# Written order over attention, four high-part buffers, rotation in single slots, ScalarE copies of turned v

## The chip, the cores and the metric

One core of a Trainium2 chip runs the whole program. The metric is the device time of one execution in microseconds (us), as the median of repeated runs. A difference of about 0.2% (3.9 us here) is what a measurement of this kernel can tell from no change.

## What is computed

One layer of a streaming encoder, on T = 320 rows: 256 of a new prompt and 64 of a running sample. D = 2048, 32 query heads and 4 key/value heads of 64, feed-forward width 5632, all float32.

```python
xn = rmsnorm(x)
u, v, q, k, va = split(xn @ w_in)            # u, v through gelu
q, k = rope(q), rope(k)                       # the first 16 of 64 dimensions
a = u * (ws @ layernorm(v) + bs)              # per chunk of 128 rows
o = sink_softmax(q @ k.T / 8, sinks) @ va     # chunks of 64 rows, window of 3 chunks
x += (sigmoid(ga) * (a @ w_branch_a) + sigmoid(gb) * (o @ w_branch_b)) @ w_out
x += (silu(h @ w_ffn_gate) * (h @ w_ffn_up)) @ w_ffn_down     # h = rmsnorm(x)
y = rmsnorm(x)
```

`ga` and `gb` are `xn @ w_gate + b_gate`, halved. Outputs are y, the new rows of k and va, and the normalised v of the sample.

## The kernel before, in words

**Blocks.** Every float32 product is made of three products of rounded parts (high by high, high by low, low by high). The weights come in blocks of 256 rows by 512 columns (512 KB). For each block SP issues a transfer into a `raw` tile (`fetch`, L127), ScalarE (ACT) rounds it into `hi` (L135), VectorE (DVE) makes `lo = raw - hi` (L144), and TensorE (PE) does 24 matmuls with 320 columns (L168 to L170), one each 0.147 us where nothing holds it up: 3.52 us a block. `hi` and `lo` have three tiles each (`PARTS`), `raw` has four (`RAWS`). While block j is multiplied, the parts of block j + 2 are made, and `raw` of block j + 6 is fetched.

**Order of the products.** First k and va (`first_gemm`, blocks 0 to 7), then from block 8, eight blocks each: q0, q1, v0, q2, v1, q3, v2, v3, gate b (gb0 to gb3), then branch b, u, gate a, branch a, the output product and the feed-forward part. The list of rows below says mm_q, mm_v, mm_gb for these.

**Calendar.** `gemm` calls `pump()` after each half block, which runs what the calendar holds for that slot (1.76 us). `later(n, fn)` books n slots ahead. After each q product `q_done` copies it to `qr` (L641), swaps the rotated rows by four small transfers on ACT's queue (`rope_swap`, L367 and L368, `swp<-qr`), rotates (`rope_turn`, L375 to L377, three DVE operations on 128x640 each, with a temporary tile of tag "st"), and splits it into `qs` (ACT L508, DVE L512, two each).

**An attend.** For each of the four groups g and the five query chunks n there is one attend, named g_n, five slots after the one before. Its steps and slots are: scores (0: PE L524, L525 into two banks `s`), peak (1: DVE `mx` L533, `nm` L535), power (2: ACT, four exponentials L546), weigh (3, 4), pack (5: DVE transpose into `u`), spread (6: SP, four transfers `pd<-u`, L577), gather (8: SP, `pf<-pd`, L586), part (11: ACT `ph` L598 and `p2` L606; 12: DVE `pl` L601, `p2` L609), values (14: PE L616 into a bank `o`), lower (15: ACT `ol` L620) and total (16: DVE L628). `pf` and `ol` take turns in the two tiles of tag "st". The page prints `p2` as `p`.

**v.** After each v product `v_done` scales it (DVE L663), applies gelu (ACT L666), turns it on PE into a bank `vt` (L671) and copies the bank into `tok`: the 256 prompt columns on DVE (L676), the 64 sample rows on ACT (L677). Statistics follow on DVE.

**Banks.** All of these share eight PSUM banks under one tag: a product holds four, an attend's scores two, its values one, each turned v one. A new tile takes a bank that the program's order has released before, and PE waits there until the last reader of that bank is done.

**Who orders.** The start, up to the end of `first_gemm`, stands under `tc.manual_schedule()`: there each engine's queue has the order in which the code was written. After that the tile framework's scheduler orders each engine's instructions within the dependences. Each engine runs its queue in order, so whatever stands ahead of an instruction is done first.

Of the kernel before, what the change touches and what calls it, by code (L numbers as in the profile page):

```python
# [10 lines left out]
F32 = mybir.dt.float32  # L11
F32R = mybir.dt.float32r
AF = mybir.ActivationFunctionType
ALU = mybir.AluOpType
# [4 lines left out]
P = 128  # L19
D = 2048  # L20
DC = D // P
T = 320
# [3 lines left out]
W = 512  # L26
# [1 line left out]
NPOS = 128 + T  # L28
WARM = 9
FILL = (6, 4)  # L30
RAWS = 4
PARTS = 3
FPARTS = (16, 16, 12)
DOWN = [
    [(0, 4), (512, 4), (1024, 4), (1536, 4)],
# [35 lines left out]
def tile_hybrid_step(ctx: ExitStack, tc: tile.TileContext, a: dict, outs: list):  # L71
    nc = tc.nc
# [6 lines left out]
    wpool = ctx.enter_context(tc.tile_pool(name="wpool", bufs=1))  # L79
# [11 lines left out]
    def later(slots, fn):  # L91
        calendar.setdefault(now[0] + max(1, slots), []).append(fn)

    startup = tc.manual_schedule()
    startup.__enter__()

    def pump():
        now[0] += 1
# [3 lines left out]
    def flush():  # L102
        while calendar:
            pump()
# [15 lines left out]
    def fetch(j, pieces=1):  # L120
        if j < len(plan):
            w, c0, k, nt = plan[j]
            raws[j] = wpool.tile([P, 2, W], F32, tag="raw", name=f"raw_{j}", bufs=RAWS)
            src = w[k * P : (k + 2) * P, c0 : c0 + nt * P].rearrange("(c p) m -> p c m", p=P)
            n = 2 // pieces
            for c in range(0, 2, n):
                nc.sync.dma_start(raws[j][:, c : c + n, : nt * P], src[:, c : c + n, :])  # L127

    def high(j, eng=None):
        if j < len(plan):  # L130
            n = plan[j][3] * P
            hi = wpool.tile([P, 2, W], F32R, tag="hi", name=f"hi_{j}", bufs=PARTS)
            parts[j] = [hi]
            if eng is None:
                nc.scalar.activation(hi[:, :, :n], raws[j][:, :, :n], AF.Copy)  # L135
            else:
                eng.tensor_copy(hi[:, :, :n], raws[j][:, :, :n])

    def low(j):
        if j < len(plan):  # L140
            n = plan[j][3] * P
            lo = wpool.tile([P, 2, W], F32R, tag="lo", name=f"lo_{j}", bufs=PARTS)
            parts[j].append(lo)
            nc.vector.tensor_tensor(  # L144
                lo[:, :, :n], raws.pop(j)[:, :, :n], f32(parts[j][0][:, :, :n]), op=ALU.subtract
            )

    def prepare(j, eng=None):
        high(j, eng)
        low(j)  # L150

    def gemm(w, c0, xh, xl, name, k0=0, nk=DC, nt=4):
        ps = [bank(f"mm_{name}_{t}") for t in range(nt)]
        for kb in range(0, nk, 2):
            j = at_block[0]
            at_block[0] += 1
            assert plan[j][1:] == (c0, k0 + kb, nt)
            ahead = j + PARTS - 1
            todo = ahead not in parts
            if todo:  # L160
                high(ahead)
            hi, lo = parts.pop(j)
            for t in range(nt):
                cols = slice(t * P, (t + 1) * P)
                for c in range(2):
                    k = kb + c
                    o = ps[t][:, :T]
                    nc.tensor.matmul(o, hi[:, c, cols], xh[:, k, :], start=(k == 0), stop=False)  # L168
                    nc.tensor.matmul(o, hi[:, c, cols], xl[:, k, :], start=False, stop=False)  # L169
                    nc.tensor.matmul(o, lo[:, c, cols], xh[:, k, :], start=False, stop=(k == nk - 1))  # L170
                if t == 1:
                    if todo:
                        low(ahead)
                    fetch(ahead + RAWS)
                if t % 2 == 1:
                    pump()
        return [p[:, :T] for p in ps]
# [9 lines left out]
    tok = main.tile([P, 3, D], F32, name="tok")  # L187
# [108 lines left out]

    def first_block():

        hi = wpool.tile([P, 2, W], F32R, tag="hi", name="hi_0", bufs=PARTS)
        lo = wpool.tile([P, 2, W], F32R, tag="lo", name="lo_0", bufs=PARTS)  # L300
        raw = raws.pop(0)
        x_in(0)
        keep_warm(FILL[0])
        nc.vector.tensor_copy(hi[:, 0, :], raw[:, 0, :])
        nc.vector.tensor_tensor(lo[:, 0, :], raw[:, 0, :], f32(hi[:, 0, :]), op=ALU.subtract)
        x_in(1)
        keep_warm(FILL[1])
        nc.scalar.activation(hi[:, 1, :], raw[:, 1, :], AF.Copy)
        nc.vector.tensor_tensor(lo[:, 1, :], raw[:, 1, :], f32(hi[:, 1, :]), op=ALU.subtract)
        parts[0] = [hi, lo]  # L310
# [1 line left out]
    first_block()  # L312
    load_x(3, nc.sync)
    fetch(3)
    fetch(4)
    prepare(1)
    x_in(2)
    fetch(5)
    for k in range(DC):
        later(k + 1, lambda k=k: x_keep(k))  # L320
        if k + 3 < DC:
# [45 lines left out]
            nc.scalar.dma_start(swp[b : b + 8, 0:nt, :], qr[b + 8 : b + 16, 0:nt, :])  # L367
            nc.scalar.dma_start(swp[b + 8 : b + 16, 0:nt, :], qr[b : b + 8, 0:nt, :])  # L368

    def rope_turn(t0):  # L370
        t1 = tmp.tile([P, 2, T], F32, tag="st", name="rope_t1")
        cb = cos_t.unsqueeze(1).broadcast_to([P, 2, T])
        sb = sin_t.unsqueeze(1).broadcast_to([P, 2, T])
        q2 = qr[:, t0 : t0 + 2, :]
        nc.vector.tensor_tensor(q2, q2, cb, op=ALU.mult)  # L375
        nc.vector.tensor_tensor(t1, swp[:, t0 : t0 + 2, :], sb, op=ALU.mult)
        nc.vector.tensor_tensor(q2, q2, t1, op=ALU.add)  # L377

    ka = ap.tile([P, 4, NPOS], F32R, name="ka")
    kl = ap.tile([P, 4, NPOS], F32R, name="kl")  # L380
# [85 lines left out]
    def first_gemm():  # L466

        ps = [bank(f"mm_kv_{t}") for t in range(4)]
        for k in range(DC):
            j, c = k // 2, k % 2  # L470
            hi, lo = parts[j]
            for t in range(4):
                cols = slice(t * P, (t + 1) * P)
                o = ps[t][:, :T]
                nc.tensor.matmul(o, hi[:, c, cols], xh[:, k, :], start=(k == 0), stop=False)
                nc.tensor.matmul(o, hi[:, c, cols], xl[:, k, :], start=False, stop=False)
                nc.tensor.matmul(o, lo[:, c, cols], xh[:, k, :], start=False, stop=(k == DC - 1))
            pump()
            if c == 1:
                parts.pop(j)  # L480
                prepare(j + 2)
                fetch(j + 2 + RAWS)
        at_block[0] = DC // 2
        return [p[:, :T] for p in ps]

    ps = first_gemm()
    startup.__exit__(None, None, None)
    for t in range(4):
        nc.scalar.activation(qr[:, t, :], ps[t], AF.Copy)
    later(1, lambda: rope_swap(2))  # L490
# [1 line left out]
    for i, n in xs:  # L492
        later(7 + i, lambda i=i, n=n: new_v(i, i * P, n))
        later(9 + 2 * i, lambda i=i: v_blocks(i))
    later(8, lambda: rope_turn(0))
    later(11, k_out)
    later(11, rope_scale)
    for g in range(4):
# [17 lines left out]
    def attend(g, n, qs, st):  # L516
# [105 lines left out]
        def total():  # L622
# [10 lines left out]
        return (  # L633
            (0, scores), (1, peak), (2, power), (3, lambda: weigh((1, 3))), (4, lambda: weigh((0, 2))),
            (5, pack), (6, spread), (8, gather), (11, lambda: part(False)), (12, lambda: part(True)),
            (14, values), (15, lower), (16, total),
        )

    def q_done(g, ps):
        for t in range(4):  # L640
            nc.scalar.activation(qr[:, t, :], ps[t], AF.Copy)  # L641
        qs = ap.tile([P, 20, 2, 64], F32R, tag="qs", name=f"qs_{g}")
        hi, lo = q_parts(g, qs)
        later(1, lambda: rope_swap(4))
        later(5, lambda: rope_turn(0))
        later(7, lambda: rope_turn(2))
        at = QK0[g]
        later(at - 5, lambda: hi(0))
        later(at - 4, lambda: lo(0))
        later(at - 3, lambda: hi(1))  # L650
        later(at - 2, lambda: lo(1))
        for n in range(5):
            for dt, step in attend(g, n, qs, {}):
                later(at + 5 * n + dt, step)
# [4 lines left out]
    def v_done(g, ps):  # L659
        vst = {}  # L660
        for t in range(4):
            v = tmp.tile([P, T], F32, tag="e1", name=f"v_{g}_{t}", bufs=4)
            nc.vector.tensor_tensor(v, ps[t], rx, op=ALU.mult)  # L663

            def curve(v=v):
                nc.scalar.activation(v, v, AF.Gelu_apprx_tanh)  # L666

            def turn(t=t, v=v):
                pt = vst[t] = bank(f"vt_{g}_{t}")
                for i, n in xs:  # L670
                    nc.tensor.transpose(pt[:n, i * P : (i + 1) * P], v[:, i * P : i * P + n], ident)  # L671

            def put(t=t):
                pt = vst.pop(t)
                c = slice((4 * g + t) * P, (4 * g + t + 1) * P)
                nc.vector.tensor_copy(tok[:, 0:2, c], pt[:, 0:256].rearrange("p (i c) -> p i c", i=2))  # L676
                nc.scalar.activation(tok[0:64, 2, c], pt[0:64, 256:384], AF.Copy)  # L677

            later(1, curve)
            later(3 + t, turn)  # L680
            later(4 + t, put)

        def stats():
            for i, n in xs:
                nc.vector.bn_stats(bst[:n, i, g, :], tok[:n, i, g * W : (g + 1) * W])

        later(9, stats)
# [57 lines left out]
        if h == 1:  # L745
            nc.vector.memset(late["wst"][64:128, :, 0:64], 0.0)

    at = 19
    later(at - 2, open_late)
    for k in range(0, DC, 2):  # L750
        later(at - 2 + k // 2 + 1, lambda k=k: split_o(k))
# [24 lines left out]
    for g in range(1, 4):  # L776
        sigmoid(gate_b, gemm(w_gate, D + g * W, xh, xl, f"gb{g}"), 80, g)
    flush()
    yh, yl = late["yh"], late["yl"]
    for g in range(4):  # L780
        ps = gemm(w_bb, g * W, yh, yl, f"bb{g}")
# [234 lines left out]
```

## Time and profile before

| | |
|---|---|
| median of 3 runs | 1955.37 us (1954.38 to 1955.47) |
| the profiled execution | 1956.22 us |
| its span | 1954.0 us, granted clock 0.995 |
| PE busy | 1931.7 us, 99% |
| DVE, ACT busy | 1042.0 us (53%), 814.3 us (42%) |
| bytes moved | 307.41 MB, mean 157 GB/s |

The span is what the trace covers; 2.2 us of the profiled execution lie around it. PE's share says that nearly the whole time is matmul time, so a change to the other engines can only win what PE spends waiting or at a lower clock. Attention runs beside PE from about 50 to 330 us; there DVE and ACT have their fullest stretches (six to eight tenths of a slice, four or five later).

### The profile page before, as it was taken

What the parts mean: (1) busy time and instruction counts of PE and PEld (TensorE: products, weight loads), DVE (VectorE), ACT (ScalarE), POOL (GpSimd) and SP (SyncE); (2) the same over time, 40 slices, a digit from 0 to 9 for tenths busy, and PEclk for the clock granted to TensorE, in tenths of its full rate; (3) what the DMA queues carried; (4) which work ended last, traced back from release to release, by engine and by line L of the source; (5) the groups of instructions that cost most, each with busy time, mean ns of one, the idle gap of its engine ahead of it and who ended that gap; (6) DMA issues with size and microseconds to landing.
All of it is one profiled execution on the core that took longest, in us unless ns stands there. A gap on an engine that the chain in (4) does not pass through costs nothing.

```text
span 1954.0 us, 31842 instructions
## 1 busy us (share of the span) xinstructions
PE 1931.7 (99%) x13201; PEld 1925.1 (99%) x13201; DVE 1042.0 (53%) x1528; ACT 814.3 (42%) x1221; POOL 4.7 (0%) x12
## 2 busy tenths in 40 slices
PE   9999999999999999999999999999999999999997
PEld 9999999999999999999999999999999999999996
DVE  6878787944355544455554444443444444444454
ACT  6666776532333343334443333333333333333343
POOL 0000000000000000000000000000000000000000
PEclk9999999999999999999999999999999999999998
DMA  8566665644444454445455555445555444555433
GB/s 278 159 172 171 171 188 174 221 157 151 151 141 132 146 148 149 149 150 205 151 148 147 149 149 151 151 151 151 149 148 148 150 151 151 151 151 149 149 128 103
DMA packets 170881, 307.41 MB, mean 157 GB/s; under 512 B 11457, under 2 KB 31377, under 8 KB 170545
## 3 DMA queue, kind: packets, MB, share of 16 engines
q1 hardware_dynamic: 166064, 295.93, 49.6%
q10 hardware_dynamic: 4672, 9.46, 1.5%
q8 instruction: 103, 1.69, 0.3%
q14 instruction: 42, 0.34, 0.0%
HBM read 292.15 MB, written 12.45 MB: 156 GB/s over the span
## 4 chain that ended last, share of the span: by engine, by line
PE 83%; ACT 1%; DVE 1%; DMA 0%; issue 0%; DVEq 0%; SPq 0%; ACTq 0%
PE mm_fg L169 5%; PE mm_fd L169 5%; PE mm_fu L169 5%; PE mm_fd L168 5%; PE mm_fu L168 5%; PE mm_fg L168 5%; PE mm_fg L170 5%; PE mm_fu L170 5%; PE mm_fd L170 5%; PE mm_u L168 2%; PE mm_ba L170 2%; PE mm_bb L169 2%; PE mm_bb L168 2%; PE mm_wo L170 2%; PE mm_ga L170 2%; PE mm_ga L168 2%
## 5 line engine op out<-in xcount | busy, mean ns | idle before, releaser
L144 DVE TENSOR_TENSOR lo<-raw,hi 128x1024 fp32r<-128x1024 f32 (+1 forms) x533 | 645.1, 1211 | 659.8 <-ACT hi L135 658.3
L135 ACT ACTIVATE hi<-raw 128x1024 fp32r<-128x1024 f32 (+1 forms) x533 | 559.2, 1050 | 1013.8 <-PE mm_fu L169 188.9
L168 PE MATMUL mm_fd<-xh,hi 128*128 128x320 f32 x704 | 218.2, 310 | 0.0
L168 PE MATMUL mm_fg<-yh,hi 128*128 128x320 f32 x704 | 217.8, 309 | 0.0
L170 PE MATMUL mm_fg<-yh,lo 128*128 128x320 f32 x704 | 217.5, 309 | 0.0
L168 PE MATMUL mm_fu<-yh,hi 128*128 128x320 f32 x704 | 217.5, 309 | 0.0
L169 PE MATMUL mm_fu<-yl,hi 128*128 128x320 f32 x704 | 217.5, 309 | 0.0
L170 PE MATMUL mm_fu<-yh,lo 128*128 128x320 f32 x704 | 217.5, 309 | 0.0
L169 PE MATMUL mm_fg<-yl,hi 128*128 128x320 f32 x704 | 217.5, 309 | 0.0
L170 PE MATMUL mm_fd<-xh,lo 128*128 128x320 f32 x704 | 217.1, 308 | 0.0
L169 PE MATMUL mm_fd<-xl,hi 128*128 128x320 f32 x704 | 217.1, 308 | 0.0
L168 PEld LDWEIGHTS mm_fg<-yh,hi 128*128 128x128 f32 x704 | 132.1, 188 | 0.1
L169 PEld LDWEIGHTS mm_fg<-yl,hi 128*128 128x128 f32 x704 | 132.1, 188 | 0.1
L170 PEld LDWEIGHTS mm_fg<-yh,lo 128*128 128x128 f32 x704 | 132.1, 188 | 0.0
L168 PEld LDWEIGHTS mm_fu<-yh,hi 128*128 128x128 f32 x704 | 132.1, 188 | 0.0
L169 PEld LDWEIGHTS mm_fu<-yl,hi 128*128 128x128 f32 x704 | 132.1, 188 | 0.0
L170 PEld LDWEIGHTS mm_fu<-yh,lo 128*128 128x128 f32 x704 | 132.1, 188 | 0.0
L169 PEld LDWEIGHTS mm_fd<-xl,hi 128*128 128x128 f32 x704 | 132.1, 188 | 0.0
L168 PEld LDWEIGHTS mm_fd<-xh,hi 128*128 128x128 f32 x704 | 132.1, 188 | 0.0
L170 PEld LDWEIGHTS mm_fd<-xh,lo 128*128 128x128 f32 x704 | 132.1, 188 | 0.0
L168 PE MATMUL mm_q<-xh,hi 128*128 128x320 f32 x256 | 81.6, 319 | 0.0
L168 PE MATMUL mm_u<-xh,hi 128*128 128x320 f32 x256 | 80.3, 314 | 0.0
(262 smaller groups left out, 3935.8 us busy)
## 6 DMA issues: line engine op xcount, KB each, us to landing
raw<-in_w_in_dram SPq DMA_DIRECT2D x103, 512.0 KB
raw<-in_w_ffn_gate_dram SPq DMA_DIRECT2D x88, 512.0 KB
raw<-in_w_ffn_up_dram SPq DMA_DIRECT2D x88, 512.0 KB
raw<-in_w_ffn_down_dram SPq DMA_DIRECT2D x82, 512.0 KB
raw<-in_w_gate_dram SPq DMA_DIRECT2D x64, 512.0 KB
raw<-in_w_branch_b_dram SPq DMA_DIRECT2D x32, 512.0 KB
raw<-in_w_branch_a_dram SPq DMA_DIRECT2D x32, 512.0 KB
raw<-in_w_out_dram SPq DMA_DIRECT2D x32, 512.0 KB
```

The lines of the kernel that those rows point to most:

```text
L135: nc.scalar.activation(hi[:, :, :n], raws[j][:, :, :n], AF.Copy)
L144: nc.vector.tensor_tensor(lo[:, :, :n], raws.pop(j)[:, :, :n], f32(parts[j][0][:, :, :n]), op=ALU.subtract)
L168: nc.tensor.matmul(o, hi[:, c, cols], xh[:, k, :], start=(k == 0), stop=False)
L169: nc.tensor.matmul(o, hi[:, c, cols], xl[:, k, :], start=False, stop=False)
L170: nc.tensor.matmul(o, lo[:, c, cols], xh[:, k, :], start=False, stop=(k == nk - 1))
```

## The change

The order as written now lasts until the gate b products end (block 104): the `manual_schedule` is left there, not after `first_gemm`. In the code that it covers the following differs.

- `hi` has four tiles, `lo` three, `raw` three. Parts are still made two blocks ahead (`AHEAD`), and a block's transfer is issued one block later than before (j + 5 instead of j + 6); the start issues one block less.
- Rotation is done in place in `swp`, and its three operations stand in slots of their own: 8, 9, 10 for k (all at 8 before) and 3, 4, 5, 5, 6, 6 after a q product (before: all three of the first half at 5, of the second at 7).
- The copy of the turned prompt columns goes from DVE to ACT.
- `total` comes two slots later (18), and the late work after v (pools, normalisation) two slots later.

Line numbers of the changed kernel are 2 or 3 higher.

```diff
-RAWS = 4
-PARTS = 3
+RAWS = 3
+HIGHS = 4
+LOWS = 3
+AHEAD = 2
...
-            hi = wpool.tile([P, 2, W], F32R, tag="hi", name=f"hi_{j}", bufs=PARTS)
+            hi = wpool.tile([P, 2, W], F32R, tag="hi", name=f"hi_{j}", bufs=HIGHS)
...
-            lo = wpool.tile([P, 2, W], F32R, tag="lo", name=f"lo_{j}", bufs=PARTS)
+            lo = wpool.tile([P, 2, W], F32R, tag="lo", name=f"lo_{j}", bufs=LOWS)
...
-            ahead = j + PARTS - 1
+            ahead = j + AHEAD
...
     fetch(3)
-    fetch(4)
     prepare(1)
     x_in(2)
-    fetch(5)
+    fetch(4)
...
-    def rope_turn(t0):
-        t1 = tmp.tile([P, 2, T], F32, tag="st", name="rope_t1")
+    def rope_ops(t0):
...
-        q2 = qr[:, t0 : t0 + 2, :]
-        nc.vector.tensor_tensor(q2, q2, cb, op=ALU.mult)
-        nc.vector.tensor_tensor(t1, swp[:, t0 : t0 + 2, :], sb, op=ALU.mult)
-        nc.vector.tensor_tensor(q2, q2, t1, op=ALU.add)
+        q2, s2 = qr[:, t0 : t0 + 2, :], swp[:, t0 : t0 + 2, :]
+        return (
+            lambda: nc.vector.tensor_tensor(q2, q2, cb, op=ALU.mult),
+            lambda: nc.vector.tensor_tensor(s2, s2, sb, op=ALU.mult),
+            lambda: nc.vector.tensor_tensor(q2, q2, s2, op=ALU.add),
+        )
...
     ps = first_gemm()
-    startup.__exit__(None, None, None)
...
-    later(8, lambda: rope_turn(0))
+    for i, op in enumerate(rope_ops(0)):
+        later(8 + i, op)
...
-            (14, values), (15, lower), (16, total),
+            (14, values), (15, lower), (18, total),
...
-        later(5, lambda: rope_turn(0))
-        later(7, lambda: rope_turn(2))
+        a, b = rope_ops(0), rope_ops(2)
+        for dt, op in ((3, a[0]), (4, b[0]), (5, a[1]), (5, b[1]), (6, a[2]), (6, b[2])):
+            later(dt, op)
...
-                nc.vector.tensor_copy(tok[:, 0:2, c], pt[:, 0:256].rearrange("p (i c) -> p i c", i=2))
+                nc.scalar.activation(tok[:, 0:2, c], pt[:, 0:256].rearrange("p (i c) -> p i c", i=2), AF.Copy)
...
-    at = 19
+    at = 21
...
     flush()
+    ordered.__exit__(None, None, None)
     yh, yl = late["yh"], late["yl"]
```

**ACT's queue around the exponentials of attend 0_4** (block 33, the first v product; `qs_1` belongs to the next group's queries, `v_0_*` to the v product). Before:

```order
L620 ACTIVATE ol_0_1_1696<-o_0_1_1675 64x512
L598 ACTIVATE ph_0_2_1731<-pf_0_2_1638 128x512
L135 ACTIVATE hi_35_1711<-raw_35_1515 128x1024
L606 ACTIVATE p2_0_2_1733<-pf_0_2_1638 64x512
L508 ACTIVATE qs_1_1253<-qr_178 64x20x64 x2
L546 ACT_TABLE_LOAD
L546 ACTIVATE pr_0_4_1766,den_0_4_1767<-s_0_4_0_1701,nm_0_4_1742 128x192 x2
```

Now:

```order
L622 ACTIVATE ol_0_1_1688<-o_0_1_1667 64x512
L137 ACTIVATE hi_35_1703<-raw_35_1547 128x1024
L600 ACTIVATE ph_0_2_1721<-pf_0_2_1630 128x512
L608 ACTIVATE p2_0_2_1723<-pf_0_2_1630 64x512
L510 ACTIVATE qs_1_1247<-qr_176 64x20x64
L548 ACT_TABLE_LOAD
L548 ACTIVATE pr_0_4_1756,den_0_4_1757<-s_0_4_0_1693,nm_0_4_1732 128x192 x2
```

One of the two `qs` copies has moved behind the exponentials; everything else that stood ahead of them still does.

**DVE's queue ahead of `lo_49`** (block 47; attend 1_4 has its peak here, and `qs_2` is the next group's). Before:

```order
L609 TENSOR_TENSOR p2_1_2_2438<-pf_1_2_2359,p2_1_2_2438 64x512
L535 SCALAR_TENSOR_TENSOR nm_1_4_2447<-mx_1_4_2444,nsink_175 128x4
L512 TENSOR_TENSOR qs_2_2103<-qr_178,qs_2_2103 64x20x64
L537 TENSOR_TENSOR es_1_4_2449<-sink_174,nm_1_4_2447 128x4
L512 TENSOR_TENSOR qs_2_2103<-qr_178,qs_2_2103 64x20x64
L555 TENSOR_TENSOR den_1_4_2468<-den_1_4_2468,es_1_4_2449 128x4
L663 TENSOR_TENSOR v_1_0_2520<-mm_v1_0_2104,rx_118 128x320
L556 RECIPROCAL den_1_4_2468<-den_1_4_2468 128x4
L144 TENSOR_TENSOR lo_49_2489<-raw_49_2272,hi_49_2475 128x1024
```

Now:

```order
L537 SCALAR_TENSOR_TENSOR nm_1_4_2435<-mx_1_4_2432,nsink_173 128x4
L539 TENSOR_TENSOR es_1_4_2437<-sink_172,nm_1_4_2435 128x4
L603 TENSOR_TENSOR pl_1_2_2452<-pf_1_2_2349,ph_1_2_2424 128x512
L611 TENSOR_TENSOR p2_1_2_2426<-pf_1_2_2349,p2_1_2_2426 64x512
L514 TENSOR_TENSOR qs_2_2095<-qr_176,qs_2_2095 64x20x64
L146 TENSOR_TENSOR lo_49_2477<-raw_49_2324,hi_49_2463 128x1024
```

Only one `qs` low part is left ahead of `lo_49`, and the first scaling of v (L663, now L666) comes behind it.

**DVE's queue around the peak of attend 2_0** (blocks 49 and 50; `mx_2_0` reads its scores, `nm_2_0` goes to its exponentials). Before:

```order
L601 TENSOR_TENSOR pl_1_3_2609<-pf_1_3_2493,ph_1_3_2573 128x512
L533 TENSOR_REDUCE mx_2_0_2612<-s_2_0_0_2581 128x2
L144 TENSOR_TENSOR lo_51_2605<-raw_51_2382,hi_51_2591 128x1024
L609 TENSOR_TENSOR p2_1_3_2575<-pf_1_3_2493,p2_1_3_2575 64x512
L533 TENSOR_REDUCE mx_2_0_2612<-s_2_0_1_2582 128x2
L535 SCALAR_TENSOR_TENSOR nm_2_0_2615<-mx_2_0_2612,nsink_175 128x4
```

Now:

```order
L146 TENSOR_TENSOR lo_51_2593<-raw_51_2422,hi_51_2579 128x1024
L603 TENSOR_TENSOR pl_1_3_2597<-pf_1_3_2483,ph_1_3_2561 128x512
L611 TENSOR_TENSOR p2_1_3_2563<-pf_1_3_2483,p2_1_3_2563 64x512
L535 TENSOR_REDUCE mx_2_0_2600<-s_2_0_0_2569 128x2
L535 TENSOR_REDUCE mx_2_0_2600<-s_2_0_1_2570 128x2
L537 SCALAR_TENSOR_TENSOR nm_2_0_2603<-mx_2_0_2600,nsink_173 128x4
```

`lo_51` has moved to the front, so `pl` waits behind it; the same five instructions stand ahead of `nm_2_0` as before. On ACT `hi_51`, for which `lo_51` waits, still stands behind `ph_1_3`, and now behind `p2_1_3` too; ahead of `ph_1_3` stand now the table load for gelu and the four gelus of v1, in one run. On SP the gather `pf_1_3` follows `raw_52` now; before, it followed `raw_53`. With three `raw` tiles `raw_52` takes the tile that `lo_49` frees, as `raw_53` did with four.

## Rows read from the trace of the kernel before

**Rows 1.** The page: busy time of each engine; the chain that ended last, by engine.

```profile
PE 1931.7 (99%) x13201; PEld 1925.1 (99%) x13201; DVE 1042.0 (53%) x1528; ACT 814.3 (42%) x1221; POOL 4.7 (0%) x12
...
PE 83%; ACT 1%; DVE 1%; DMA 0%; issue 0%; DVEq 0%; SPq 0%; ACTq 0%
```

**Rows 2.** PE's waits: waiting line, releaser: us in total, times, longest us.

```profile
PE vt L671 <- ACT pr L546: 3.5, 3, 2.5
PE o L616 <- ACT pr L546: 2.0, 1, 2.0
...
PE s L524 <- DVE qs L512: 0.5, 1, 0.5
PE o L616 <- DVE p L609: 0.2, 1, 0.2
```

**Rows 3.** PE's timeline at 144 us: start, duration, operation [idle before <-releaser].

```profile
147.01 0.90 PE L671 MATMUL vt<-ident,v 128*128 128x128 f32 x3 [2.55 <-ACT pr L546]
```

**Rows 4.** PE's timeline at 215 us.

```profile
217.03 0.50 PE L616 MATMUL o<-ph,vv 128*128 128x512 f32 x1 [2.02 <-ACT pr L546]
```

**Rows 5.** Windows: length, busy us of each engine (instructions), granted clock, DMA share, GB/s.

```profile
147.01:150.08 3.07, 3.07 (x13) 3.03 (x13) 2.97 (x8) 3.02 (x11) 0.00 (x0) 0.51 0.43 128
160.00:163.07 3.07, 3.07 (x21) 2.94 (x20) 2.30 (x7) 2.56 (x9) 0.00 (x0) 1.00 0.81 261
217.03:221.30 4.27, 4.26 (x19) 4.04 (x20) 3.22 (x9) 3.82 (x14) 0.00 (x0) 0.65 0.28 73
20.00:30.00 10.00, 9.80 (x70) 9.54 (x69) 6.52 (x12) 6.48 (x13) 0.00 (x0) 1.00 0.98 324
```

**Rows 6.** ACT's timeline at 130 to 147 us (attend 0_4's exponentials at its end).

```profile
130.07 0.63 ACT L598 ACTIVATE ph<-pf 128x512 fp32r<-128x512 f32 x1 [2.28 <-DMA pf<-pd]
132.21 0.42 ACT L546 ACTIVATE pr<-s,nm 128x192 f32<-128x192 f32 x1 [1.51 <-DVE nm L535]
...
141.99 2.55 ACT L508 ACTIVATE qs<-qr 64x1280 fp32r<-64x1280 f32 x2
144.75 1.28 ACT L546 ACT_TABLE_LOAD   x1 [0.21 <-DVE nm L535]
146.05 0.42 ACT L546 ACTIVATE pr<-s,nm 128x192 f32<-128x192 f32 x1
```

**Rows 7.** DVE's timeline at 200 to 215 us (attends 1_3, 1_4, 2_0).

```profile
200.74 1.49 DVE L512 TENSOR_TENSOR qs<-qr,qs 64x1280 fp32r<-64x1280 f32 x1
...
202.45 1.49 DVE L512 TENSOR_TENSOR qs<-qr,qs 64x1280 fp32r<-64x1280 f32 x1
...
204.53 1.19 DVE L144 TENSOR_TENSOR lo<-raw,hi 128x1024 fp32r<-128x1024 f32 x1
...
214.72 0.16 DVE L535 SCALAR_TENSOR_TENSOR nm<-mx,nsink 128x4 f32<-128x4 f32 x1
```

**Rows 8.** SP's queue at 206 us.

```profile
205.76 0.39 SPq L127 DMA_DIRECT2D raw<-in_w_in_dram  x1
206.33 0.85 SPq L586 DMA_DIRECT2D pf<-pd  x2
```

**Rows 9.** ACT's timeline at 204 to 216 us.

```profile
202.89 1.06 ACT L135 ACTIVATE hi<-raw 128x1024 fp32r<-128x1024 f32 x1
203.97 1.28 ACT L666 ACT_TABLE_LOAD   x1
...
210.81 0.63 ACT L598 ACTIVATE ph<-pf 128x512 fp32r<-128x512 f32 x1 [1.73 <-DMA pf<-pd]
...
216.28 0.31 ACT L546 ACTIVATE pr<-s,nm 128x64 f32<-128x64 f32 x1
```

**Rows 10.** Groups by line, 8 to 560 us: count | busy us, mean ns | idle before, releaser.

```profile
L375 DVE TENSOR_TENSOR qr<-qr,cos_t 128x640 f32<-128x640 f32 x9 | 7.3, 813 | 1.2 <-DMA swp<-qr 1.2
...
L676 DVE COPY tok<-vt 128x256 f32<-128x256 f32 x16 | 6.6, 416 | 0.1
...
L428 ACT ACTIVATE kout<-pk 128x256 f32<-128x256 f32 x1 | 0.4, 359 | 0.0
```

More of the change, by code (lines that the diff above doesn't have):

```diff
@@ L92, in later @@
         calendar.setdefault(now[0] + max(1, slots), []).append(fn)
-    startup = tc.manual_schedule()
-    startup.__enter__()
+    ordered = tc.manual_schedule()
+    ordered.__enter__()
     def pump():
@@ L297, in first_block @@
     def first_block():
-        hi = wpool.tile([P, 2, W], F32R, tag="hi", name="hi_0", bufs=PARTS)
-        lo = wpool.tile([P, 2, W], F32R, tag="lo", name="lo_0", bufs=PARTS)
+        hi = wpool.tile([P, 2, W], F32R, tag="hi", name="hi_0", bufs=HIGHS)
+        lo = wpool.tile([P, 2, W], F32R, tag="lo", name="lo_0", bufs=LOWS)
         raw = raws.pop(0)
@@ L480, in first_gemm @@
                 parts.pop(j)
-                prepare(j + 2)
-                fetch(j + 2 + RAWS)
+                prepare(j + AHEAD)
+                fetch(j + AHEAD + RAWS)
         at_block[0] = DC // 2
```

## The prediction

> **What bounds the kernel now.** I read the page's busy times and chain first: PE is busy 99% of the span and is 83% of the chain that ended last, the other engines about 1% each [rows 1]. So the time is the matmuls, and a change to the order can only win what PE loses between them. PE's waits come second: the reader is to see that nearly all of them have one releaser, the exponentials of an attend (L546), on which a turned v (vt) or the values (o) wait for a bank [rows 2]. That list gives 3.5 + 2.0 + 0.5 + 0.2 = 6.2 us in the part that the change touches.
>
> Third, PE's timeline at the two long ones: 2.55 us at 144 us (call it A) and 2.02 us at 215 us (B) [rows 3, 4]. Fourth, windows behind them. The 3.07 us after A had a granted clock of 0.51 and 13 matmul entries, where the same length has 21 at clock 1.00; the 4.27 us after B had 0.65 [rows 5]. That is the lower of the engine's two levels, 1.2 GHz instead of 2.4, after PE had been idle for over 2 us; the loss is 3.07 x 0.49 = 1.5 us after A and 4.27 x 0.35 = 1.5 us after B. A thus costs 2.55 + 1.5 = 4.05 us, B 2.02 + 1.5 = 3.5 us, the other four waits (3.5 - 2.55) + 0.5 + 0.2, about 1.7 us. In all some 9.3 us can be won, and no more, since outside attention nothing else changes for PE.
>
> Fifth, the queues of ACT and DVE ahead of A and B, to see what made the exponentials late. For A: ACT was busy without a break from 132.21 to 144.54 (141.99 + 2.55), then waited 0.21 for nm, loaded a table for 1.28, began the exponentials at 146.05, and PE went on at 147.01, 0.96 later [rows 3, 6]. For B the start was a late transfer: lo_49 stood on DVE behind two low parts of 1.49 each, started at 204.53 and ended near 205.7; only then could SP issue the raw tile that takes its place (205.76) and behind it the gather (206.33) [rows 7, 8]. ACT sat idle 1.73 until that gather landed at 210.81, nm came at 214.72, and the exponentials at 216.28 [rows 7, 9].
>
> **The change part by part, against the profiled execution's 1956.22 us.**
>
> *A.* PE is due at 147.01 - 2.55 = 144.46. In the written order the bank of attend 0_4's first two scores goes to the v tile turned one half block earlier, vt_0_1, so PE is due about 1.76 + 0.25 us sooner, at 142.45 (12 matmuls of 0.147, by 21 in 3.07 us [rows 5], and the turn). On ACT one of the two qs copies goes behind the exponentials: half of 2.55, 1.27 [rows 6]. The idle 1.51 ahead of 132.21 can take the next weight block's high part, about 1.0 [rows 6, 9]. So the table load starts 1.3 to 2.3 us earlier than 144.75, the exponentials 1.28 after that, PE 0.96 later: 144.7 to 145.7, and PE idles 2.3 to 3.2 us. If the gather at 130.07 also came without its 2.28 of idle time [rows 6], the lower end would be 0. I take 2.3, the lower end of the rows' own range, because nm also loses an operation ahead of it (the low part of p). With 1.5 at the low clock A is 3.8 us, a gain of 0.25 us (bounds: gain 4.05, loss 0.7).
>
> *B.* Three things make it earlier: one low part of 1.49 leaves the queue ahead of lo_49, a scaling of v too, and the gather stands behind one raw transfer less. Its high part ended at 203.95 [rows 9], 0.6 ahead of it, and has one qs copy (1.27) less ahead now; so lo_49 starts 0.6 to 1.9 us sooner, and the gather is issued that much sooner. Two things hold it back: the gelus of v1 with their table load, 1.28 [rows 9], now stand in one run ahead of ph, and pl waits behind lo_51, so that a high part, 1.06 [rows 9], lies between ph and nm: about 5.0 us instead of 214.72 - 210.81 = 3.9 [rows 7, 9]. Of the gain at the gather between 0 and 0.8 us is left at nm. I take 0.5, in between: idle 1.5. That lies between no idle time, which loses nothing at the clock, and B's 2.02, which lost 1.5; I take 1.0, nearer B. B becomes 2.5, a gain of 1.0 us (bounds: gain 3.5, loss 0.7).
>
> *Small waits.* Each is shorter than one or two of the operations that change places ahead of it (a low part 1.19, a qs part 1.49 [rows 7]), so each may go or grow. The wait on the low p (0.2 [rows 2]) goes, since p now stands ahead of the peaks; new ones may come where k's rotation ends two slots later and where v's scaling stands behind lo. I take 1.3 for 1.7, a gain of 0.4 (bounds: gain 1.7, loss 1.2, one low part).
>
> *The copies of v.* 16 copies of 0.416 leave DVE, 6.6 us [rows 10]. On ACT the nearest row is the copy of kout from a bank, same 128x256, 0.359 [rows 10]: 16 x 0.36 = 5.7 us added there. They stand behind the exponentials of A and B, and ACT's idle time later in the slot covers them; without that cover one copy delays a bank by 0.36. Nothing in the sum.
>
> *Rotation.* Same operations, two slots (3.5 us) sooner after the swap's transfers, on which DVE now waits 1.2 us over all of them [rows 10]. DVE may wait up to 3.5 us more for each of three q products, with the peaks of an attend queued behind; there PE's allowance is whole blocks, so 0 in the sum, with 0 to 2 us kept for the range.
>
> *Buffers.* One raw tile less means each transfer is issued one block (3.5 us) later. In steady state it was waiting for its use that long. At the start the transfers run near capacity (share 0.98, PE 9.80 of 10 us busy [rows 5]): 0 in the sum, up to one block, 3.5 us, for the range. The fourth high tile lets ACT's rounding begin a block sooner and costs nothing.
>
> *Late work* two slots later lies under the gate products: 0.
>
> Sum: -0.25 - 1.0 - 0.4 = -1.65, which gives 1954.6 us for the profiled execution. That execution is 0.85 above the median of the runs (1955.37), so the forecast is **1953.7 us**.
>
> A rule against the change: ACT goes into the exponentials of A with no gap now. In rows, a table load behind a busy ACT begins at 203.97, 0.02 after the high part that ends at 203.95 [rows 9], and takes 1.28; nothing is waited for between them. The Trainium skill, "ScalarE: Activation LUTs", section "What ACT_TABLE_LOAD costs", gives 1283 ns for the load, as the rows do, and about 1380 ns of drain besides, which the rows don't show. By the page the sum would be 1.4 us higher, since A's exponentials would start that much later.
>
> **The rivals.**
>
> *Both long waits go* (chance 0.22). In favour: ACT is idle 2.28, 1.51 and 1.73 us in their chains [rows 6, 9], time that another order can use. Against: A would need its exponentials 3.6 us sooner than 146.05 and I find 1.3 to 2.3. Price: 4.05 + 3.5 + 0.4 gone, **1947.4 us**.
>
> *The gathers come late* (0.13, the slower side). Written queues can't step around a late transfer. With three raw tiles each raw waits on SP for a lo, and the gather behind it in the same queue; ACT's ph, with the next high part behind it, then waits. If the gathers slip by one slot, 1.76 us, at five attends (0_4, 2_0 and the three small waits on banks and queries), A becomes 2.3 + 1.76 + 1.5 = 5.6, B 1.5 + 1.76 + 1.5 = 4.8, each small one 0.5 + 1.76 + 1.5 = 3.8 instead of 0.5. That is 1.5 + 1.3 + 9.9 = 12.7 more than before: **1968 us**. It decides for "slower" from a slip of about 1.1 us at all five (5 x 1.1 = 5.5, less the 1.65 won). Against: SP's order has the gather nearer the front.
>
> *Trade* (0.12): PE's own order is practically the same, A and B keep their length, and new waits at k's rotation or v's scaling eat the small gain: **1955.4 us**.
>
> *Drain on the path* (0.03): the pause above exists where ACT comes busy into a load: 1953.7 + 1.4 = **1955.1 us**. That the page says so is its only support; the row at 203.97 speaks against it.
>
> **How the numbers follow.** My forecast, A about as long, B shorter, has 0.50; its own range is 1950 to 1957. About 0.13 of that lies under 1951.5, the bound from which a measurement tells faster (0.2%, 3.9 us), and 0.01 above 1959.3. Faster: 0.22 + 0.13 = 0.35. Slower: 0.13 + 0.01 = 0.14. Same: 0.51. The range goes down to 1946.5, so that the first rival is in, and up to 1959.5, which takes in the bounds of rotation and start; the late gathers stay outside.
>
> **What would show it.** PE's waits should list a vt on the exponentials of about 2.3 us near 142 to 145 us, with a window at clock 0.5 behind it, and an o near 215 us of 1 to 2 us. The gather of 1_3 should be issued at 204 to 205 us. The L375 operations should wait longer for swp, and the group of the copy of v stand on ACT at 0.3 to 0.4 us. Wrong it would be if A is gone, if a wait on a raw transfer (hi released by a DMA) stands in PE's list, if the start loses more than a microsecond, or if new waits over 1 us appear in other attends.

## The result, and the profile after

The changed kernel takes 1964.70 us (median of 4 runs, 1963.65 to 1964.94) against 1954.88 us for the kernel before beside it: 9.8 us slower, ratio 1.0049 with a 95% interval of 1.0037 to 1.0061. The profiled execution took 1964.72 us, its span grew from 1954.0 to 1962.9. The page's busy times and chain, to be set beside [rows 1]:

```profile
PE 1935.5 (99%) x13201; PEld 1927.3 (98%) x13201; DVE 1044.8 (53%) x1512; ACT 821.4 (42%) x1237; POOL 4.7 (0%) x12
...
PE 90%; DVE 4%; ACT 3%; DMA 1%; issue 1%; SPq 0%; ACTq 0%; DVEq 0%
```

DVE and ACT are hardly busier, but their share of the chain went from 1% each to 4% and 3%. PE's waits, beside [rows 2], say where:

```profile
PE vt L674 <- DVE f L630: 3.1, 1, 3.1
PE vt L674 <- ACT pr L548: 3.1, 1, 3.1
PE s L526 <- DVE qs L514: 1.7, 1, 1.7
PE pk L427 <- DVE qr L378: 1.2, 1, 1.2
...
PE o L618 <- DVE f L630: 1.1, 1, 1.1
PE mm_q L172 <- DVE lo L146: 1.0, 2, 0.7
```

The list was nearly all exponentials; now most releasers are DVE operations: value sums (f), a low part of queries (qs), k's rotation (qr), a weight's low part (lo).

Where the time went is read by following one instruction of PE in both traces. A matmul of four attends' values, the same four in both kernels, in the kernel before:

```profile
125.32 0.39 PE L616 MATMUL o<-p,vv 128*128 128x512 f32 x1
203.82 0.39 PE L616 MATMUL o<-ph,vv 128*128 128x512 f32 x1
261.95 0.39 PE L616 MATMUL o<-ph,vv 128*128 128x512 f32 x1
339.18 0.39 PE L616 MATMUL o<-ph,vv 128*128 128x512 f32 x1
```

And after:

```profile
129.08 0.40 PE L618 MATMUL o<-p,vv 128*128 128x512 f32 x1
208.75 0.39 PE L618 MATMUL o<-ph,vv 128*128 128x512 f32 x1
268.29 0.39 PE L618 MATMUL o<-ph,vv 128*128 128x512 f32 x1
348.13 0.39 PE L618 MATMUL o<-ph,vv 128*128 128x512 f32 x1
```

The lag is 3.8 us at the first of them, ahead of A (the product matmuls have it already by 92 us, at the end of the first query product), 4.9 behind A, 6.3 behind B and 8.95 at the end, which is the growth of the span. So four places lose: the first query product 3.8, A 1.2 more than before, B 1.4 more, and the rest 2.6, most of it at one wait. PE's timeline of the three long waits in attention and windows behind them (columns as in [rows 5]):

```profile
149.66 0.66 PE L674 MATMUL vt<-ident,v 128*128 128x128 f32 x3 [3.13 <-ACT pr L548]
221.37 0.63 PE L674 MATMUL vt<-ident,v 128*128 128x128 f32 x3 [3.14 <-DVE f L630]
274.32 0.30 PE L526 MATMUL s<-ka,qs 128*128 128x64 f32 x1 [1.67 <-DVE qs L514]
```

```profile
149.66:153.59 3.93, 3.93 (x18) 3.89 (x19) 2.26 (x4) 3.88 (x11) 0.00 (x0) 0.57 0.33 97
221.37:225.00 3.63, 3.63 (x16) 3.63 (x16) 0.55 (x1) 3.46 (x15) 0.00 (x0) 0.54 0.45 111
274.32:279.50 5.18, 5.18 (x27) 5.18 (x28) 3.46 (x4) 2.40 (x4) 0.00 (x0) 0.69 0.73 213
```

Each is followed by a stretch at the lower clock level (0.57, 0.54, 0.69 granted on average), which costs 1.7, 1.7 and 1.6 us beside the idle time: 4.8, 4.8 and 3.3 us in all.

What held B is in DVE's timeline of the changed kernel:

```profile
217.01 1.22 DVE L146 TENSOR_TENSOR lo<-raw,hi 128x1024 fp32r<-128x1024 f32 x1 [1.51 <-ACT hi L137]
218.15 0.68 DVE L603 TENSOR_TENSOR pl<-pf,ph 128x512 fp32r<-128x512 f32 x1
218.87 0.68 DVE L611 TENSOR_TENSOR p<-pf,p 64x512 fp32r<-64x512 f32 x1
219.58 0.49 DVE L535 TENSOR_REDUCE mx<-s 128x2 f32<-128x128 f32 x2
220.11 0.16 DVE L537 SCALAR_TENSOR_TENSOR nm<-mx,nsink 128x4 f32<-128x4 f32 x1
...
220.38 0.84 DVE L630 TENSOR_TENSOR f<-o,ol 64x256 f32<-64x256 f32 x2
```

DVE stood idle 1.51 us for the high part of a weight block that PE wants two blocks later. Behind that low part stood, in the written order, the parts of p, the peak and the value sum, and PE's turned v waited for the bank that the sum reads. ACT meanwhile waited for nm:

```profile
220.37 1.28 ACT L548 ACT_TABLE_LOAD   x1 [3.39 <-DVE nm L537]
```

### The profile page after: what moved, and what is told of

It reads as the page before. It is cut to its first block, busy times and chain, and to the rows that moved or that the text cites. A ratio compares the mean times of both kernels' runs of the same rounds, so it can differ in the third digit from the quotient of the medians.

```text
span 1962.9 us, 32087 instructions
## 1 busy us (share of the span) xinstructions
PE 1935.5 (99%) x13201; PEld 1927.3 (98%) x13201; DVE 1044.8 (53%) x1512; ACT 821.4 (42%) x1237; POOL 4.7 (0%) x12
## 4 chain that ended last, share of the span: by engine, by line
PE 90%; DVE 4%; ACT 3%; DMA 1%; issue 1%; SPq 0%; ACTq 0%; DVEq 0%
PE mm_fu L172 5%; PE mm_fd L171 5%; PE mm_fd L172 5%; PE mm_fg L172 5%; PE mm_fu L171 5%; PE mm_fg L171 5%; PE mm_fg L170 5%; PE mm_fu L170 5%; PE mm_fd L170 5%; PE mm_u L170 2%; PE mm_ba L171 2%; PE mm_bb L172 2%; PE mm_ba L170 2%; PE mm_bb L170 2%; PE mm_wo L170 2%; PE mm_ga L171 2%
## 5 line engine op out<-in xcount | busy, mean ns | idle before, releaser
L172 PE MATMUL mm_q<-xh,lo 128*128 128x320 f32 x256 | 80.7, 315 | 1.0 <-DVE lo L146 1.0
```

## The experiments

Theory P says that the loss is several waits, each made by one part. Rival O says that the written order costs whatever stands in it. The differences below are to the kernel before in the same comparison, in which the changed kernel stands at +9.8 us. Some of what follows is smaller than the 3.9 us that a measurement can tell from no change: a difference of 2 or 3 us between two experiments is a sign, not a size. Where the executions of two kernels do not overlap, the text takes the sign as shown.

**1. The written order alone** (`e5`). The order stays, and the rotation in place; the rest is undone.

```diff
-RAWS = 3
-HIGHS = 4
+RAWS = 4
+HIGHS = 3
...
-            (14, values), (15, lower), (18, total),
+            (14, values), (15, lower), (16, total),
...
-    at = 21
+    at = 19
```

(and `fetch(5)` at the start, rotation at slots 8, 5 and 7, the copy of v on `nc.vector`).

> The changed kernel with everything undone but the written order and the rotation in place: buffers 4 raw, 3 high, 3 low; rotation in the slots of before; copies of v on VectorE; value sums at slot 16, late work two slots sooner. Theory P (parts): the 9.8 us lost are five separate waits, each made by one part of the change, so this kernel is near the one before, 1954 to 1957 us, with two long waits as before. Rival O (order): queues in the written order are the loss whatever stands in them, so 1962 to 1966 us.

It took 1974.67 us, +20.3 (ratio 1.0104, 1.0087 to 1.0121). Theory P fell: the order is the loss, even more than O said. The other parts of the change together win 10.5 us back under it. Its waits differ; most are values waiting for the low part of p:

```profile
PE o L619 <- DVE pl L604: 7.2, 5, 2.9
PE s L527 <- DVE qs L515: 2.6, 1, 2.6
PE o L619 <- ACT pr L549: 2.1, 1, 2.1
```

**2. Everything but the written order** (`e6`).

```diff
     ps = first_gemm()
+    ordered.__exit__(None, None, None)
...
-    ordered.__exit__(None, None, None)
```

> The changed kernel with the written order left after the first product, as before; buffers, rotation, copies and later sums stay changed. Theory P: the scheduler can step around some of the waits but the sums at slot 18 and three raw tiles still cost, 1957 to 1961 us. Rival O: as before, 1954 to 1956 us.

It took 1954.03 us, -0.3 (0.9991 to 1.0010). O was right: buffers, rotation, copies and later sums together change nothing under the scheduler. With them in place the order costs about 10 us.

**3. The parts, one at a time, under the order.** Sums at slot 16 (`e1`), the edit being that one number:

> The changed kernel with the value sums back at slot 16. Theory P: the 3.1 us wait of a turned v on a value sum near 218 us goes and leaves the wait on the exponentials behind it, about 2; the 1.05 us wait of values on a sum near 294 us goes; the wait on the queries' low part near 274 us falls from 1.7 to 0.9, with less time at the low clock. 1961 to 1963 us. Rival O: 1964 to 1966 us, the waits only change their names.

It took 1962.20, +7.8, so the two slots cost about 2 us (its executions, 1961.41 to 1962.75, lie under those of the changed kernel, 1963.65 to 1964.94). The wait on the sum at B went, and one on the exponentials took its place (o, 2.3 us, the longest of its list). A's 3.1 us became 0.7 on a sum and 1.2 on the exponentials. New waits of 1.4 us (values on the low part of p, at 197 us) and 1.1 us (scores on v's scaling, at 284 us) took a part of the gain, as rival O had it.

The buffers of before (`e2`):

> The changed kernel with 4 raw, 3 high and 3 low tiles again and the fifth transfer at the start. Theory P: ScalarE no longer waits for weights at 84 to 96 us (2.0, 1.1 and 0.6 us in the changed kernel), PE's waits on high and low parts there go, 2.4 us, so 1962 to 1963 us. Rival O: 1964 to 1966 us.

It took 1966.99, +12.6: 2.8 us worse (1966.29 to 1969.29, over every execution of the changed kernel). At 82 us the same waits on high and low parts stand as with three raw tiles (0.7 the longest), and PE is 3.5 us late at 100 us instead of 3.8, so scarce raw tiles make little of the loss there, 0.3 to 0.4 us. What three raw and four high tiles win comes later; the run does not part the two.

Rotation in the slots of before (`e3`):

> The changed kernel, written order kept, with the rotations back in the slots of before (k: all at 8; queries: 5 and 7, three operations in a row), still in place. The base under the written order ran 20 us over the kernel before and the whole change 9.8, so the other parts together give back 10. Theory R: single slots for the rotation give back most of it, by keeping the six 0.8 us operations out of VectorE's queue ahead of the low parts and the queries' parts: 1968 to 1973 us. Rival V: the copies of v do, and the rotation is worth little: 1963 to 1966 us, with the 1.2 us wait of PE on k's rotation near 65 us gone.

It took 1964.71, +10.1, no difference, within rival V's range. The wait on k's rotation went, and the waits on high and low parts at 74 to 84 us grew by as much; the queries' wait in the last group grew from 1.7 to 2.6 us, A's fell to 2.3.

The copy of v on DVE (`e4`):

> The changed kernel, written order kept, with the copies of v back on VectorE. Theory V: VectorE's queue in v's products fills up, waits of the values on the low parts of the weights' p and of a turned v on copies return: 1968 to 1973 us. Theory R: 1964 to 1967 us.

It took 1968.33, +13.8: the copies on ACT are worth 3.9 us under the order. R fell, and V's time holds. V's waits are there only in part (values on the low part of p 1.1 us, a turned v on the copies 0.2); the longest new one is a product's 1.6 us on v's scaling (L666).

Alone, the buffers win 2.8 us and the copies 3.9, the rotation nothing, and the later sums lose 2.0: about 5 of the 10.5 us that the parts win together. The rest is in how they work together or in the late work two slots later, which no run undid by itself.

**4. Where in the program the order loses** (`e7`): scheduler's order in the first query product, written order from the second.

```diff
     for c, g in QV:
+        if (c, g) == ("q", 1):
+            ordered = tc.manual_schedule()
+            ordered.__enter__()
```

(and left after `first_gemm`).

> The changed kernel with the scheduler's order during the first query product (the blocks 8 to 15) and the written order again from the second on. Theory P: the losses at 65 us (PE waits 1.2 us for k's rotation) and at 78 to 95 us (2.5 us, high and low parts late behind k's parts and the swap) belong to the written order of that stretch and go: 1960 to 1962 us. Rival: all of the loss is made in attention, the stretch only moves it: 1964 to 1966 us.

It took 1960.45, +5.9: that stretch costs 3.9 us, by which the trace of the changed kernel was late there; the rest, 5.9 us, is lost behind it.

**5. The low part and the transfer behind the calendar's work** (`e8`).

```diff
+                if t % 2 == 1:
+                    pump()
                 if t == 1:
                     if todo:
                         low(ahead)
                     fetch(ahead + RAWS)
-                if t % 2 == 1:
-                    pump()
```

> The changed kernel with one pair of lines turned round in the block: the calendar's work of the first half block is written ahead of the low part and the transfer, not behind them. Theory L: in the written order a low part that waits for its high part (1.2 us near 144 us, 1.5 us near 216 us) holds the peaks and value sums behind it on VectorE. Near 216 us ScalarE was idle 3.4 us for that, so the wait of a turned v there falls from 3.1 to about 0.5 with its time at the low clock; near 146 us ScalarE itself was busy to 0.3 us before, so little is won there. 1959 to 1961 us. Rival: the low parts, now later, hold PE or the transfers instead: 1964 us or more.

It took 1959.01, +4.3 (1.0015 to 1.0036): 5.5 us won by turning the calendar's call and the block's own work round. That work is the low part and the transfer (`fetch`), so the run does not part what DVE's queue wins from what SP's wins. DVE's timeline at A now, where in the changed kernel the low part stood ahead of the peak and waited 1.17 us:

```profile
143.22 1.02 DVE L535 TENSOR_REDUCE mx<-s 128x2 f32<-128x384 f32 x2 [0.95 <-PE s L527]
144.27 0.16 DVE L537 SCALAR_TENSOR_TENSOR nm<-mx,nsink 128x4 f32<-128x4 f32 x1
144.47 0.16 DVE L539 TENSOR_TENSOR es<-sink,nm 128x4 f32<-128x4 f32 x1
144.55 1.22 DVE L146 TENSOR_TENSOR lo<-raw,hi 128x1024 fp32r<-128x1024 f32 x1
```

The peak waits only for the scores. At A I had expected little, since ACT was busy; A's wait fell from 3.1 to 0.5: ACT's whole run ahead of the exponentials was sooner (its load for the gelus began at 139.13 instead of 140.51, and the exponentials at 147.07 instead of 148.69), while PE arrived 1.0 later. The gather of attend 0_1, for which ACT waits ahead of these, was issued at 129.96 instead of 131.44, with PE 1.4 us later. B's wait is 1.7, on the exponentials, not the 0.5 expected. The rival is right in one place: in the first query product, waits on low parts grew (1.4 us the longest), and PE was 5.1 us late at 100 us instead of 3.8. Behind it this kernel is faster than the one before: at 345 us it is 2.6 us late.

**6. Together.** Low part behind and scheduler in the first product (`e10`):

> As the last, and with the scheduler's order during the first query product. Theory L: the two gains add, 1955 to 1957 us. Rival: 1960 us or more.

It took 1954.87, +0.1. The gains add: 3.9 and 5.5 alone, 9.7 together.

Scheduler in the first product and sums at 16 (`e12`):

> The scheduler's order during the first query product, written order from the second on, value sums at slot 16. Parts add: 1960.5 less 2.5, 1957 to 1959 us. Rival: the sums at 16 only helped what the first product's delay had pushed together, 1960 to 1961 us.

It took 1959.37, +4.6, against +5.9 with the sums at 18. The executions overlap (1958.65 to 1960.37, 1959.62 to 1960.97), so that the sums win anything here is not shown.

All three (`e11`):

> All three: scheduler during the first query product, calendar ahead of the low part, value sums at slot 16. Theory L: the wait on a sum near 215 us is gone in either of two ways, so the two do not add: 1954 to 1957 us, the long wait near 144 us and the queries' part of the last group being left. Rival: 1958 us or more.

It took **1948.97 us**, -5.8, ratio 0.9972 (0.9963 to 0.9982): the best version, ahead of both kernels, and outside what either theory said: the gains more than add. Against `e10` the sums at 16 win 5.9 us. In `e10` no wait on a sum's bank is left; its longest wait is that of a product for a bank that v's scaling reads:

```profile
206.40 0.41 PE L170 MATMUL mm_q<-xh,hi 128*128 128x320 f32 x1 [2.25 <-DVE v L667]
```

A value sum stands ahead of that scaling on DVE in `e10` (201.33 to 202.18), and no longer in `e11`, where the wait is gone; between 205 and 240 us PE gains 3.5 us on `e10`, the largest part of the 5.9. The sum's own length is 0.85 of that wait's 2.25 us; what made the rest is open. The longest of PE's waits in the whole program are now these:

```profile
PE s L527 <- DVE qs L515: 1.1, 1, 1.1
PE warm L224 <- DVE eps L187: 1.1, 1, 1.1
PE pss_y L949 <- DVE acc L895: 1.0, 1, 1.0
PE o L619 <- ACT pr L549: 0.2, 1, 0.2
```

The same without the order and with the sums at 16 (`e9`):

> The changed kernel without the written order over attention and with the value sums at slot 16. Theory P: the 2.2 us wait of a turned v on a sum near 213 us goes with its time at the low clock, 1950 to 1952 us, under the kernel before. Rival: the wait on the exponentials stands right behind it, 1953 to 1955 us.

It took 1954.91, +0.3 (0.9993 to 1.0011), the rival: the sum's wait went, and the waits on the exponentials grew to 5.2 us in two (in the traced execution, the slowest of ten with 1957.79). What the sums at 16 give in `e11` they don't give under the scheduler alone. The scheduler's order with the calendar ahead of the low part was not run, so it is not shown that only a written order can reach the best time.

**7. What costs about 4 us in the first query product.** ACT's timeline of the changed kernel there:

```profile
80.06 1.09 ACT L643 ACTIVATE qr<-mm_q 128x320 f32<-128x320 f32 x3 [0.86 <-DVE kl L413]
81.19 1.06 ACT L137 ACTIVATE hi<-raw 128x1024 fp32r<-128x1024 f32 x1
...
84.00 2.01 ACT L137 ACTIVATE hi<-raw 128x1024 fp32r<-128x1024 f32 x2 [1.75 <-DMA swp<-qr]
88.03 1.06 ACT L137 ACTIVATE hi<-raw 128x1024 fp32r<-128x1024 f32 x1 [2.02 <-DMA raw<-in_w_in_dram]
```

High parts stand behind copies that wait for k's parts (0.86), and behind the swap (1.75); the last one waits for its transfer (2.02), where `e2` with four raw tiles won 0.3 to 0.4 us for PE. Theory K: k's parts are booked too late (`e13`).

```diff
-        later(12 + g, lambda g=g: put_new_k(g))
+        later(9 + g, lambda g=g: put_new_k(g))
```

(and k's rotation all at slot 8.)

> The changed kernel, written order throughout, with k's rotation back in slot 8 and the new k parts booked three slots earlier (9 + g instead of 12 + g). Theory K: the 3.8 us lost by 100 us come from the calendar putting k's 32 part operations so late (72 to 80 us) that ScalarE's copies of the first query product wait for them and the high parts behind those copies and the swap come late; now 1 us or less is lost there, 1961 to 1962.5 us. Rival S: the four swap transfers on ScalarE's queue hold the high parts whatever stands ahead of them: 1963.5 to 1966 us.

It took 1966.20, +11.7, at the upper end of S's range. K fell: PE was 6.8 us late by 125 us (0.6 of it from the start, before the products) instead of 3.8, with one wait of 2.6 on a high part at 75 us. That k's parts, nearer to one another, crowd both queues is likely, but not shown.

The order throughout with the two other repairs (`e15`):

> The changed kernel, written order throughout, with the calendar ahead of the low part and the sums at slot 16. If the first query product's loss adds to the rest as with the low part alone (1959.0 and 1954.9), this is 4 us over the best so far: 1952 to 1954 us. If not, 1950 us or less.

It took 1953.72, -0.8, 5.0 us over the best version: the first query product's loss adds, as expected.

The same with k early (`e14`):

> The last with k early as in the first. Theory K: it comes to the best so far without any stretch of scheduler's order, 1948 to 1950.5 us. Rival S: 1952 us or more.

It took 1956.49, +2.0: worse again, with one wait of 4.3 us on a low part. That the stretch's written order costs 4 to 5 us is shown by `e7` against the changed kernel (3.9), `e10` against `e8` (4.1) and `e11` against `e15` (5.0); which of its steps does is open. Neither raw tiles (`e2`), nor the rotation's slots (`e3`), nor late k parts (`e13`) make it by themselves. A swap off ACT's queue was not tried.

## Why the prediction was wrong

It forecast 1953.7 us with no difference as the likeliest case; it took 1964.7 us, 9.8 us slower and outside the range. One of its signs of being wrong came, new waits over 1 us in other attends (274 and 294 us). Against the sum:

- **The step that failed first is the bound, "outside attention nothing else changes for PE", with "0 in the sum" for rotation and buffers.** I priced only places where PE waited before. The written order took away the scheduler's stepping aside everywhere, and the first query product, without one wait before, lost 3.8 us: 1.2 for k's rotation, the rest around high and low parts that came late (1.2 of it in waits that a list shows). The small-waits term had named k's rotation as a place for a new wait and still came out 0.4 lower than before. The buffers by themselves were no loss (`e2` without them is 2.8 us slower).
- **B: predicted an idle time of 1.5 on the exponentials, 2.5 us in all; measured 3.14 on a value sum, 4.8 us.** The gather did come sooner, as put: it was issued at 210.45 with PE 5.3 us later than before, some 1.2 us sooner on PE's clock than 206.33. But PE came sooner as well, which I had put at A only: it stopped at 218.23 (221.37 less 3.14), which is 212.9 with the 5.3 us taken off, against 215.0 before: 2.1 us sooner, and at a turned v instead of the values. And the part "total two slots later" has no term at all in my sum. I followed it as late work and did not ask which bank it holds, nor what stands ahead of it on DVE; PE's turned v waited for that bank. I had seen that lo_51 stands in front and waits for its high part, and counted it for nm only. `e1`, with the sum at 16, takes the wait on the sum away and leaves 2.3 on the exponentials; `e8`, with the low part behind, leaves 1.7.
- **A: predicted 2.3 idle, 3.8 us; measured 3.13, 4.8 us.** The mechanism was right: PE came sooner (1.7 us on its clock, 2.0 put) and waited for the same exponentials. The size was off: 3.13 lies in the 2.3 to 3.2 that my rows gave, and I took the lower end. A high part did fill the idle time ahead of the exponentials of 0_3, as I had it, but these began at 136.59, 4.4 us later than before [rows 6] with PE 3.8 later; then ACT waited 0.33 us for the sums of the powers (den), and 0.27 for nm, since the low part ahead of the peak had waited 1.17. So the exponentials of 0_4 came 1.1 us sooner on PE's clock (148.69 against 146.05), not 1.3 to 2.3.
- **Small waits: 1.3 predicted; measured at the queries 1.67 and 1.6 more at the low clock, a sum 1.05, p 0.25.** A value sum stands between the queries' two low parts there (270.93, 0.84 us); with it at slot 16 the wait is 1.1 (`e1`). I had priced such waits without the clock.
- **Copies of v: 0 predicted; they win 3.9 us under the order** (`e4`), at 0.379 each (0.36 taken). The rotation's wait for the swap is the second line:

```profile
L679 ACT ACTIVATE tok<-vt 128x256 f32<-128x256 f32 x16 | 6.1, 379 | 0.7 <-PE vt L674 0.6
...
L376 DVE TENSOR_TENSOR qr<-qr,cos_t 128x640 f32<-128x640 f32 x9 | 7.3, 822 | 3.2 <-DMA swp<-qr 3.2
```

- **Rotation:** the wait for the swap grew from 1.2 to 3.2 us, as forecast, and costs PE nothing that shows (`e3`, with the slots of before, takes the same time).
- **The rivals.** The slower one, late gathers, is right in part. Ahead of B the gather came sooner. Ahead of A the gather of 0_1 came 1.8 us late on PE's clock (131.44 with PE 3.8 later, before 125.90). The transfer in front of it on SP was 1.7 us late; it was issued as a low part ended that had itself waited, and ACT waited for the gather:

```profile
128.97 1.23 DVE L146 TENSOR_TENSOR lo<-raw,hi 128x1024 fp32r<-128x1024 f32 x1 [2.00 <-ACT hi L137]
130.22 0.39 SPq L129 DMA_DIRECT2D raw<-in_w_in_dram  x1
131.44 0.34 SPq L588 DMA_DIRECT2D pf<-pd  x1
134.99 0.63 ACT L600 ACTIVATE ph<-pf 128x512 fp32r<-128x512 f32 x1 [2.04 <-DMA pf<-pd]
```

Three raw tiles are not the ground that the rival took them for: with four (`e2`) that gather is as late (131.29). Its general ground, that a written queue cannot step around something late, was right; at B, at the queries and in the first query product the late things are weights' parts and sums, not transfers. "Trade" named k's rotation rightly, but not the size. The first rival, both long waits gone, did not happen. The drain behind a table load, which the Trainium skill's "ScalarE: Activation LUTs" has in "What ACT_TABLE_LOAD costs", does not show here either: behind a busy ACT the load begins at 212.14, takes 1.28, and the gelu begins at 213.44; behind a wait, the load at 220.37 takes 1.28 and the exponentials begin at 221.66.

## What to carry to other kernels

When an order is written by hand, put work that only feeds later blocks (here the low parts, needed two blocks on, with their transfers) behind the work that the critical engine waits for in the same slot; an in-order queue turns a harmless wait of the former into a wait of the latter. The same turn cost a little over 1 us in the first query product, so it is to be tried stretch by stretch. Price such a change by walking every queue for instructions that wait, also where nothing waited before, and for each step that comes later ask which buffer it releases. Judge an order and its tuning together: the same parts won nothing under the scheduler and 10 us under the written order; and the order lost 10 us or, tidied and begun one product later, won 5.8 us on the kernel before.

## What was not expected of the hardware

The fall of the clock does not follow the length of the idle time alone. After 1.23 us of idle time at 65 us, and 1.05 at 294, the changed kernel's windows show a granted clock of 1.00:

```profile
65.44:69.00 3.56, 3.56 (x26) 3.56 (x27) 3.16 (x8) 3.24 (x8) 0.00 (x0) 1.00 0.18 26
294.04:298.00 3.96, 3.96 (x27) 3.77 (x28) 2.63 (x6) 3.91 (x14) 0.00 (x0) 1.00 0.56 166
```

In the best version 1.11 us, at 260 us, was followed by 0.68:

```profile
260.56:264.00 3.44, 3.40 (x18) 3.43 (x19) 3.40 (x5) 1.11 (x2) 0.00 (x0) 0.68 0.49 147
```

So a wait of little over 1 us cost its own length in two places and, with 3.44 x 0.32 = 1.1 us more, twice its length in the third. What decides is open.
